# Tail columns scaled on ScalarE and summed by transposes in PSUM, with 384 dense cells a head and an exponential ranking of the keys

## The chip, the cores and the metric

The kernel runs on one core of a Trainium2 chip, in one launch. The metric is the device time of a run in microseconds. The kernel before took 1063.42 us, the median of three runs (1061.2 to 1066.42). Engines are named as in the profile: PE is TensorE (matmuls and transposes) with its weight load PEld, DVE is VectorE, ACT is ScalarE, POOL is GpSimd (it issues the gathers), SP is SyncE (it issues the other transfers).

## The reference

One encoder layer works on 512 tokens of width 1024, all in float32. A mixer comes first (windowed attention and latent attention side by side, with norms that a conditioning vector modulates); the change leaves it alone. Then comes PEER, a retrieval over 128 x 128 experts of one neuron each, and a last RMSNorm. PEER, per token `x` (after its norm), with 8 heads and two halves `p` of the query:

```
q     = (x @ w_query)                       # 8 heads x 2 halves x 128
s     = q . sub_keys[head, half]            # 128 scores for each half
top_s, top_i = top_k(s, 16)                 # 16 keys of each half
cand  = top_s[0][:, None] + top_s[1]        # 256 pairs; pair (i, j) is expert 128 i + j
best_s, idx  = top_k(cand, 16)              # 16 experts a head, 128 a token
g     = softmax(best_s)
out   = sum over head, k of  g * gelu(x . expert_u[idx]) * expert_v[idx]
x     = x + g_f * out ;  result = rmsnorm(x, final_norm)
```

A row of `expert_u` with its row of `expert_v` is 8 KB.

## The kernel before

**Dense and tail.** Which expert a token wants is known only at run time, and 512 x 128 pairs of token and expert are too many to gather one by one. Some experts are wanted by many tokens, so the kernel ranks the 128 keys of each half by how often they lie high, and takes a fixed staircase of ranks, `RECTS` (L32), as the dense cells: key ranks `a0` to `a1` of one half with the first `w` ranks of the other. That makes 512 cells, experts, a head. They are computed for all 512 tokens by matmul: each head has 4 chunks (`NCH`) of 128 experts. What a token wants outside the cells is its tail.

**Ranking** (`rank1` to `rank3`, L1198 to L1245). Before a head's scores exist, `rank1` scores the first 128 tokens only (L1204), takes each token's eighth largest score with VectorE's max, and marks the keys at or above it; `rank2` counts the marks by matmuls with ones (L1213, L1215), compares the counts pair by pair into ranks, and turns ranks into a permutation matrix `pm`; `rank3` permutes the keys (L1231) and stores the table of expert ids and the ids of the cells.

**Routing** (`route`, L1427). Written out by hand as one list of steps, in which the head `i` is scored, head `i+1` is ranked, head `i+2` gets its query, and head `i-1` has its weights made: the dense weights `dexp` of 512 cells for each token, masked, transposed (L1419) and stored to DRAM as `gts`, and the other pairs as a list of expert code and weight a token (`cdgs`, in DRAM `cdg`). `dn(k)` in it pulls one step of the dense work. `start_routing` (L1004) opens it: it ranks head 0 among the transposes that write the tokens to DRAM (`rows`, L1010, operation `tt<-ident,x1T` L1014), and runs head 1's query. At the end the tokens are sorted by the length of their tails.

**Dense work** (`dense`, L1497). A generator. For each chunk: gather 128 rows of u (`du`), transpose them in four 128x128 pieces (`turn`, L1522), round them to a high part `uh` (ScalarE, L1525) and a correction `ul` (`low`: L1532, then ScalarE L1533), 24 matmuls into `udot` (`dots`, L1540), gelu (ScalarE, L1545), times the weights `gT` (VectorE, L1553). Once the first chunk of the next head is through, `outputs` of a head (L1579) multiplies its 4 chunks of weights with its 4 gathered `dv` into `vacc` (L1591), 4 token blocks by 2 halves of 512 columns, and VectorE adds each to `accd` (L1565). `vacc` has two banks of PSUM pool `PD[0]` and, in the tail stage, one of `PD[1]`.

**Tail.** Sorted tokens make four blocks of 128. Column `j` of a block is the `j`-th tail expert of each of its tokens, `TAIL` (L37) says how many columns a block gets, and tokens with more pairs put the rest on rows of a shared block "fold" of 4 columns, which `fold_rows` (L1704) lays out and a matmul with `fold` brings home (`begin`, L1939). That is 81 columns. For each: GpSimd looks up 128 ids (`tid`) and gathers 128 rows of 8 KB into one of 6 buffers `tuv` (L156 from `tail_id` and `tail_load`). Then, with the gate found by L1882:

```
L1891  DVE  dot of tuv[:, 0:D] with the tokens hp        (tail_col)
L1811  ACT  gelu of the dot          (flush, one column later)
L1812  ACT  times the gate: wg
L1813  DVE  tacc = tuv[:, D:] * wg + tacc
```

At a block's end `add_tail` multiplies `tacc` by the layer gate `gf` (L2015), adds the residual rows `x1` (L2016) and scatters to DRAM `zs`. When the last block and the last head's outputs are done, `finish` (L2071) loads `zs`, joins it to `accd` (L2081), norms and stores.

**What sets the order.** In the tail stage each engine keeps the order in which the program issues (`in_order`, L1087). `interleave` (L1102) decides it: each step of `dense` adds its TensorE cost (`PE_CHUNK`, `PE_OUT`) to a meter, and columns are loaded (`t.load`) or worked (`t.col`) as their costs (`DM_COL`, `VE_COL`) fall due, at `RATE` 1.05 of an even spread. The steps that routing took are subtracted. `t.load` runs up to 5 columns ahead.

Of the kernel before, what the change touches and what calls it, by code (L numbers as in the profile page):

```python
# [31 lines left out]
RECTS = ((0, 2, 60), (2, 6, 31), (6, 14, 20), (14, 32, 6))  # L32
# [4 lines left out]
TAIL = (29, 21, 16, 11)  # L37
FOLD = 4
MOST = 56
# [19 lines left out]
PE_OUT = 3.43  # L59
# [4 lines left out]
VE_COL = 2.9  # L64
# [857 lines left out]
def peer(tc, A, G, DR, out, xpool):  # L922
    nc = tc.nc
    with ExitStack() as ctx:
# [55 lines left out]
        with ExitStack() as c2:  # L980
# [3 lines left out]
            G.vbufs.append(1)  # L984
# [19 lines left out]
def start_routing(tc, G, H):  # L1004

    nc = tc.nc
    with tc.tile_pool(name="h2p", bufs=1, side="right") as W:
# [9 lines left out]

        H[0].rank1()
        rows(0)
        H[0].rank2()  # L1020
        rows(1)
# [80 lines left out]
def interleave(t, dense, ready, used):  # L1102
# [21 lines left out]
    for p, d, v in dense:  # L1124
        load += p * rd - d
        vec += p * rv - v
        while (load > 0 or vec > 0) and t.ncol < NTAIL:
            if (load > 0 or t.nuv - t.ncol < 2) and t.nuv < min(NTAIL, t.ncol + len(t.uv) - 1):
# [13 lines left out]
    while t.ncol < NTAIL:  # L1142
        if t.nuv < min(NTAIL, t.ncol + len(t.uv) - 1):
            t.load()
# [7 lines left out]
def route_setup(tc, A, G, R):  # L1152
    nc = tc.nc
    G.onesb = R.tile([128, 128], BF16, name="onesb")
    nc.vector.memset(G.onesb, 1.0)
# [4 lines left out]
    G.noff = R.tile([128, 258], F32, name="noff")  # L1160
    iota(nc, G.noff[:, 0:256].rearrange("p (a b) -> p a b", a=2), [[0, 2], [1, 128]])
    iota(nc, G.noff[:, 256:258], [[0, 2]], cm=1)
# [5 lines left out]
class Head:  # L1168
# [28 lines left out]

    def rank1(self):  # L1198
        nc, R = self.nc, self.R
        pss = self.G.PS.tile([128, 2, 128], F32, name="pss", tag="rank")  # L1200
        m8 = R.tile([128, 2, 8], F32, name="m8s", bufs=2)
        self.ind = R.tile([128, 2, 128], BF16, name="ind", bufs=1)
        for p in range(2):
            nc.tensor.matmul(pss[:, p], self.q[p][:, 0:128], self.keys[:, 0, p], start=True, stop=True)  # L1204
        for p in range(2):
            nc.vector.max(m8[:, p], pss[:, p])
        for p in range(2):
            nc.vector.tensor_scalar(self.ind[:, p], pss[:, p], m8[:, p, 7:8], None, op0=OP.is_ge)

    def rank2(self):  # L1210
        nc, R, G = self.nc, self.R, self.G
        psc = G.PS.tile([128, 258], F32, name="psc", tag="rank")
        nc.tensor.matmul(psc[:, 0:256], G.onesb, self.ind.rearrange("p a b -> p (a b)"), start=True, stop=True)  # L1213
        for p in range(2):
            nc.tensor.matmul(psc[:, 256 + p:257 + p], self.ind[:, p], G.onesb[:, 0:1], start=True, stop=True)  # L1215
        key = R.tile([128, 258], F32, name="pkey", bufs=1)
# [898 lines left out]
```

## Time and profile before

| | us |
|---|---|
| runs | 1061.2, 1063.42, 1066.42 |
| profiled execution | 1053.43 |
| its span | 1051.6 |
| TensorE busy (89%) | 940.5 |
| VectorE busy (76%) | 794.0 |
| GpSimd busy (51%) | 534.5 |
| ScalarE busy (40%) | 424.5 |

The mean granted clock of TensorE is 0.961. HBM was read for 187.95 MB at 197 GB/s over the span with the writes. The span is one execution's time from first to last instruction, and the profiled execution's own time lies 1.8 us above it. The mixer takes the first 330 us or so; routing runs from there to 597 us; dense chunks and tail columns share the time from 597 to 1006 us; the last join and norm follow. Busy TensorE is not TensorE at its peak, as matmuls are pipelined and their ends are modelled: a group's mean there is more than the distance from one to the next.

### The profile page before, as it was taken

Reading aid. Unit: us, or ns where it says so; the run is one execution under the profiler, and the core shown is the slowest. Engines: PE = TensorE matmul, PEld = TensorE weight load, DVE = VectorE, ACT = ScalarE, POOL = GpSimd, SP = SyncE. Lnnn points to the kernel's source line nnn. Section 1 sums busy time; section 2 is a strip of 40 time slices with the busy share of each in tenths; the row PEclk is TensorE's granted clock in tenths of the full one; section 3 lists DMA queues with packets and bytes.
Section 4 is the critical chain, followed back from the end, with each engine's and each line's share of the span. In section 5 each row is a group of like instructions: output and inputs, shape, how many; then the busy total and the mean of one; then the engine's idle time right before and its main releaser. Section 6 shows DMA issues by size and latency. Waiting matters only on the chain.

```text
span 1051.6 us, 13224 instructions
## 1 busy us (share of the span) xinstructions
PE 940.5 (89%) x4046; PEld 619.5 (59%) x4046; DVE 794.0 (76%) x2284; ACT 424.5 (40%) x921; POOL 534.5 (51%) x553
## 2 busy tenths in 40 slices
PE   7898989998999898999878878999998999969992
PEld 2475648776898545666554454563746666555641
DVE  4628566889637379999999587998677886866987
ACT  2333366656414335577764332231413323122312
POOL 1145611324322144666665547687578857675513
PEclk9999899999999998999988989999999999989996
DMA  8554132422211643554325669977689869786542
GB/s 317 208 227 166 55 113 86 174 82 90 81 41 60 218 148 101 161 143 123 98 60 131 214 244 313 344 249 256 243 310 389 315 228 337 271 304 238 169 175 82
DMA packets 77189, 198.94 MB, mean 189 GB/s; under 512 B 23286, under 2 KB 41078, under 8 KB 64886
## 3 DMA queue, kind: packets, MB, share of 16 engines
q0 software_dynamic: 26400, 118.93, 31.6%
q1 hardware_dynamic: 49992, 78.50, 22.5%
q8 instruction: 32, 0.52, 0.2%
q10 hardware_dynamic: 720, 0.62, 0.2%
q14 instruction: 45, 0.37, 0.1%
HBM read 187.95 MB, written 18.96 MB: 197 GB/s over the span
## 4 chain that ended last, share of the span: by engine, by line
PE 59%; DVE 23%; DMA 6%; issue 5%; ACT 3%; POOL 2%; another core or an unknown queue 0%; SPq 0%; ACTq 0%; DVEq 0%; POOLq 0%
PE vacc L1591 13%; PE udot L1540 12%; PE q L1191 8%; PE proj L305 4%; PE outp L305 4%; PE ops L831 3%; DMA tuv<-in_UV,tid 3%; PE ut L1522 2%; PE sc L807 2%; DVE tscr L1891 2%; PE adar L352 1%; DVE tacc L1813 1%; PE pt L815 1%; PE ut L1532 1%; DMA wraw_pq<-in_w_pq 1%
## 5 line engine op out<-in xcount | busy, mean ns | idle before, releaser
L1591 PE MATMUL vacc<-dv,gT 128*128 128x512 f32 x512 | 229.2, 605 | 7.0 <-DVE accd L1565 5.7
L1591 PEld LDWEIGHTS vacc<-dv,gT 128*128 128x128 f32 x512 | 98.5, 194 | 129.8 <-issue 114.3
L1813 DVE SCALAR_TENSOR_TENSOR tacc<-tuv,twg,tacc 128x1024 f32<-128x1024 f32 x81 | 103.7, 1280 | 35.1 <-ACT twg L1812 28.0
L1891 DVE SCALAR_TENSOR_TENSOR tscr<-tuv,thp 128x1024 bf16<-128x1024 f32 x81 | 98.8, 1220 | 32.8 <-DMA tuv<-in_UV,tid 24.4
L156 POOL DMA_INDIRECT tid<-tab,tci x81 | 98.5, 1216 | 29.5 <-issue 23.0
L156 POOL DMA_INDIRECT tuv<-in_UV,tid x81 | 97.9, 1208 | 29.1 <-issue 16.4
L1540 PE MATMUL udot<-hH,uh 128*128 128x512 f32 x256 | 109.8, 429 | 0.0
L1540 PE MATMUL udot<-hH,ul 128*128 128x512 f32 x256 | 104.1, 407 | 0.0
L1540 PE MATMUL udot<-hL,uh 128*128 128x512 f32 x256 | 103.6, 405 | 0.0
L1191 PE MATMUL q<-hx,wraw_pq 128*128 128x512 f32 x208 | 95.8, 602 | 0.0
L1811 ACT ACTIVATE twg<-tdots 128x1 f32<-128x1 f32 x81 | 16.4, 202 | 140.1 <-DVE tscr L1891 124.7
L327 POOL TENSOR_TENSOR ada_acc<-ada_acc,ada_w 128x1024 f32<-128x1024 f32 x9 | 21.5, 2384 | 81.5 <-ACT ada_w L326 28.6
L297 POOL TENSOR_TENSOR wl_in<-wraw_in,wh_in 128x1024 fp32r<-128x1024 f32 x10 | 25.9, 2590 | 70.5 <-ACT wh_in L296 70.3
L1191 PEld LDWEIGHTS q<-hx,wraw_pq 128*128 128x128 f32 x208 | 38.2, 193 | 37.3 <-issue 36.9
L809 ACT ACTIVATE psb<-psb,anm 128x512 f32<-128x512 f32 (+2 forms) x64 | 41.0, 641 | 46.1 <-DVE psb L808 31.3
L1533 ACT CAST ul<-ut 128x512 fp32r<-128x512 f32 x64 | 37.4, 585 | 53.9 <-PE ut L1532 36.6
L1525 ACT CAST uh<-ut 128x512 fp32r<-128x512 f32 x64 | 37.3, 584 | 52.3 <-PE ut L1522 32.5
L1540 PEld LDWEIGHTS udot<-hH,ul 128*128 128x128 f32 x256 | 49.7, 194 | 12.5 <-issue 0.2
L1540 PEld LDWEIGHTS udot<-hH,uh 128*128 128x128 f32 x256 | 50.1, 196 | 9.4 <-issue 1.2
L1540 PEld LDWEIGHTS udot<-hL,uh 128*128 128x128 f32 x256 | 50.0, 195 | 9.4 <-issue 0.2
L156 POOL DMA_INDIRECT dv<-in_UV,cid x32 | 40.7, 1271 | 25.0 <-PE vacc L1591 16.9
L1532 PE MATMUL ut<-uh,nident 128*128 128x512 f32 x64 | 29.5, 461 | 24.3 <-issue 11.6
(402 smaller groups left out, 2211.9 us busy)
## 6 DMA issues: line engine op xcount, KB each, us to landing
ada_w<-in_w_ada SPq DMA_DIRECT2D x22, 1024.0 KB
wraw_pq<-in_w_pq SPq DMA_DIRECT2D x16, 512.0 KB
gts<-gts SPq DMA_DIRECT2D x32, 256.0 KB
gT<-gts SPq DMA_DIRECT2D x32, 256.0 KB
wraw_in<-in_w_in SPq DMA_DIRECT2D x10, 512.0 KB
wraw_out<-in_w_out SPq DMA_DIRECT2D x8, 512.0 KB
x1T<-in_xT SPq DMA_DIRECT2D x4, 512.0 KB
ada_w<-in_w_ada SPq DMA_DIRECT2D x4, 512.0 KB
```

The costliest lines, as they stand in the source:

```text
L156: nc.gpsimd.indirect_dma_start(out=out, out_offset=None, in_=src, in_offset=bass.IndirectOffsetOnAxis(ap=idx, axis=0), **kw)
L305: nc.tensor.matmul(ps, a[:, c], b[:, c], start=n == 0, stop=n == 3 * kc - 1)
L809: nc.scalar.activation(U.p, U.p, AF.Exp, bias=nm, scale=-1.0, accum_out=B.den[:, i:i + 1])
L831: nc.tensor.matmul(B.ops[U.grp][:, U.h], U.pt[:, j], vr, start=j == 0, stop=j == U.nk - 1)
L1191: nc.tensor.matmul(self.q[p][:, cols], w[:, c], x[:, c, cols], start=c == 0, stop=c == KC - 1)
L1525: nc.scalar.copy(uh, pt)
L1532: nc.tensor.matmul(pt, G.nident, uh, start=False, stop=True, skip_group_check=True)
L1533: nc.scalar.copy(ul, pt)
L1540: nc.tensor.matmul(ps, a, b[:, k], start=k == 0 and i == 0, stop=k == KC - 1 and i == 2)
L1591: nc.tensor.matmul(ps, ws[h, k][:, b * 128:(b + 1) * 128], vs[k][:, sl], start=k == 0, stop=k == NCH - 1)
L1813: nc.vector.scalar_tensor_tensor(acc, uv[:, D:], wg, acc, op0=OP.mult, op1=OP.add)
L1891: nc.vector.scalar_tensor_tensor(B.s, uv[:, 0:D], 1.0, B.hp, op0=OP.mult, op1=OP.mult, accum_out=B.dots[:, c])
```

## The change

Four things are changed together.

1. `RECTS` now has five steps and 384 cells a head, so `NCH` is 3: 24 dense chunks in all, and three products instead of four in each `vacc`. `TAIL` becomes 34, 26, 20, 14, with 4 fold columns as before: 98 columns, and up to 64 pairs a token.
2. The ranking. `rank0` scores all 512 tokens against the 128 keys of a half in one product, keys on partitions, and ScalarE takes the exponential with the sum over the tokens (`stat`). `rank1` reads the sum's bits as an integer, shifts it, and subtracts a small offset to part ties; `rank2` turns the copies of the keys to rows by two transposes and ranks as before. The max, the marks and the counting matmuls are gone.
3. The sums of the tail. `flush` has ScalarE multiply the gathered v half in place by `wg`; one column later `sum_late` turns its eight 128x128 pieces on TensorE into two PSUM banks `tsum`, which add up a block's columns (transposed). Only the 4 fold columns keep VectorE's accumulation. At a block's end `end_sums` copies the eight pieces with the gate `gfc` on ScalarE, turns them back on TensorE into the `vacc` banks, and VectorE adds the result to the residual rows. Fold rows come home by eight 128-column products a block, into the same banks.
4. What follows from it: `vacc` has only the two banks of `PD[0]`; there are 7 buffers `tuv`, with the same lead of 5; the next head's u are loaded earlier; the costs `PE_OUT` and `VE_COL` are 2.6 and 2.1; `rank2` stands behind `dn(1)`.

```diff
-RECTS = ((0, 2, 60), (2, 6, 31), (6, 14, 20), (14, 32, 6))
+RECTS = ((0, 2, 45), (2, 6, 23), (6, 14, 12), (14, 25, 6), (25, 45, 2))
-TAIL = (29, 21, 16, 11)
+TAIL = (34, 26, 20, 14)
-MOST = 56
+MOST = 64
-PE_OUT = 3.43
+PE_OUT = 2.6
-VE_COL = 2.9
+VE_COL = 2.1
...
+        H[0].rank0(0)
+        rows(0)
+        H[0].rank0(1)
+        rows(1)
         H[0].rank1()
-        rows(0)
         H[0].rank2()
-        rows(1)
         H[0].rank3()
...
+    def rank0(self, p):
+        ps = self.G.PS.tile([128, T], F32, name="pst", tag="rank")
+        nc.tensor.matmul(ps, self.keys[:, 0, p], self.q[p], start=True, stop=True)
+        nc.scalar.activation(junk, ps, AF.Exp, scale=KEYSCALE, accum_out=self.stat[:, p:p + 1])
...
+        nc.vector.tensor_scalar(bits, self.stat.bitcast(I32), KEYBITS, None, op0=OP.arith_shift_right)
+        nc.vector.tensor_tensor(self.key, bits, G.noff, op=OP.subtract)
...
-                i = 0 if len(G.PD) == 1 or (b * 2 + hh) % 3 else 1
-                ps = G.PD[i].tile([128, 512], F32, name="vacc", bufs=G.vbufs[i])
+                ps = G.PD[0].tile([128, 512], F32, name="vacc", bufs=2)
...
-    for uv, wg, dot, gate, acc in t.pending:
+    for uv, wg, dot, gate, acc, pe in t.pending:
         nc.scalar.activation(wg, dot, AF.Gelu)
         nc.scalar.activation(wg, wg, AF.Copy, scale=gate)
-        nc.vector.scalar_tensor_tensor(acc, uv[:, D:], wg, acc, op0=OP.mult, op1=OP.add)
+        if pe:
+            nc.scalar.activation(uv[:, D:], uv[:, D:], AF.Copy, scale=wg)
+            t.late.append((uv, acc))
+        else:
+            nc.vector.scalar_tensor_tensor(acc, uv[:, D:], wg, acc, op0=OP.mult, op1=OP.add)
...
+def sum_late(nc, G, t):
+    for uv, S in t.late:
+        for hh in range(2):
+            for k in range(4):
+                o = D + (hh * 4 + k) * 128
+                nc.tensor.matmul(S.ps[hh][:, k], uv[:, o:o + 128], G.ident, is_transpose=True, start=not S.open and k == 0,
...
     nc.vector.scalar_tensor_tensor(B.s, uv[:, 0:D], 1.0, B.hp, op0=OP.mult, op1=OP.mult, accum_out=B.dots[:, c])
+    if t.late:
+        sum_late(nc, t.G, t)
     flush(nc, t)
...
+    for k in range(KC):
+        nc.scalar.activation(turned[:, k], S.ps[k // 4][:, k % 4], AF.Copy, scale=G.gfc[:, k:k + 1])
+    yield
+    G.flush_adds()
+    back = [G.PD[0].tile([128, 4, 128], F32, name="tback", tag="vacc", bufs=2) for _ in range(2)]
+    for k in range(KC):
+        nc.tensor.transpose(back[k // 4][:, k % 4], turned[:, k], G.ident)
+    yield
+        nc.vector.tensor_tensor(x1[:, sl], x1[:, sl], back[hh].rearrange("p j t -> p (j t)"), op=OP.add)
```

On TensorE the start of routing stood so before. `pss` are the scores of 128 tokens for the ranking of head 0, `tt` the turned tokens, `psk` the permuted keys, `q` the query of head 1, `sps` the scores of head 0:

```order
L1204 MATMUL pss<-keys,qsb 128x128 x2
L1014 MATMUL tt<-ident,x1T 128x128 x8
...
L1014 MATMUL tt<-ident,x1T 128x128 x4
L1231 MATMUL psk<-pm,keys 128x128 x2
L1014 MATMUL tt<-ident,x1T 128x128 x4
L1232 MATMUL psk<-prow,pm 128x1
L1233 MATMUL psk<-pm,prow 128x128
L1191 MATMUL q<-x1T,wraw_pq 128x512 x4
L1263 MATMUL sps<-kp,qsb 128x128 x4
```

There after the change, from the first `tt` on (`pst` are the ranking scores of all tokens; the first `pst` stands just ahead):

```order
L1017 MATMUL tt<-ident,x1T 128x128 x4
L1193 MATMUL q<-x1T,wraw_pq 128x512
L1017 MATMUL tt<-ident,x1T 128x128 x4
L1206 MATMUL pst<-qsb,keys 128x512
L1017 MATMUL tt<-ident,x1T 128x128 x4
L1193 MATMUL q<-x1T,wraw_pq 128x512
L1017 MATMUL tt<-ident,x1T 128x128 x4
L1224 MATMUL psc<-ident,pkeyb 128x128 x2
L1193 MATMUL q<-x1T,wraw_pq 128x512 x2
L1238 MATMUL psk<-pm,keys 128x128 x2
```

Head 1's query now stands in pieces between the steps of head 0's ranking, and the first of them ahead of the second rank product.

At the outputs of the first head of the tail stage, TensorE's order was, from the last dots of the chunk on:

```order
L1540 MATMUL udot<-hH,uh 128x512
L1540 MATMUL udot<-hL,uh 128x512
L1540 MATMUL udot<-hH,ul 128x512
L1591 MATMUL vacc<-dv,gT 128x512 x32
L1522 MATMUL ut<-ident,du 128x128 x4
```

And it is now, at the same place (the number of `tuv` is that of its buffer):

```order
L1549 MATMUL udot<-hH,uh 128x512
L1549 MATMUL udot<-hL,uh 128x512
L1549 MATMUL udot<-hH,ul 128x512
L1837 MATMUL tsum<-ident,tuv_5684 128x128 x8
L1599 MATMUL vacc<-dv,gT 128x512 x3
L1837 MATMUL tsum<-ident,tuv_5685 128x128 x8
L1599 MATMUL vacc<-dv,gT 128x512 x3
L1837 MATMUL tsum<-ident,tuv_5686 128x128 x8
L1599 MATMUL vacc<-dv,gT 128x512 x3
```

An output has three products instead of four, and the eight transposes of a column stand between one output and the next.

At the last head's outputs, behind which TensorE has nothing left to do, stood `vacc<-dv,gT` x32 in one piece, from the last dots on:

```order
L1540 MATMUL udot<-hL,uh 128x512
L1540 MATMUL udot<-hH,ul 128x512
L1591 MATMUL vacc<-dv,gT 128x512 x32
L987 TENSOR_LOAD nit
L988 COMPARE_AND_BRANCH
```

Now the last three columns' transposes and those that turn the last sums back (`tback`) stand behind the first output:

```order
L1549 MATMUL udot<-hH,ul 128x512
L1837 MATMUL tsum<-ident,tuv_5684 128x128 x8
L1599 MATMUL vacc<-dv,gT 128x512 x3
L1837 MATMUL tsum<-ident,tuv_5685 128x128 x8
L1837 MATMUL tsum<-ident,tuv_5686 128x128 x8
L1837 MATMUL tsum<-ident,tuv_5687 128x128 x8
L2061 MATMUL tback<-ident,tturn 128x128 x8
L1599 MATMUL vacc<-dv,gT 128x512 x21
L990 TENSOR_LOAD nit
```

Seven of the eight outputs wait behind the last columns.

## Rows read from the trace of the kernel before

**Rows 1.** The chain that ended last, by engine, whole span.

```profile
PE 59%; DVE 23%; DMA 6%; issue 5%; ACT 3%; POOL 2%; another core or an unknown queue 0%; SPq 0%; ACTq 0%; DVEq 0%; POOLq 0%
```

**Rows 2.** Stretches of the span, busy time of each engine; columns by the header.

```profile
core 0: us, PE busy (x) PEld busy (x) DVE busy (x) ACT busy (x) POOL busy (x), PEclk, DMA share, GB/s
428.00:521.00 93.00, 92.98 (x406) 60.31 (x405) 89.36 (x507) 63.80 (x118) 55.83 (x105) 1.00 0.51 143
521.00:597.00 76.00, 57.53 (x217) 34.05 (x215) 67.27 (x294) 43.98 (x75) 45.17 (x75) 0.89 0.38 103
...
597.00:1005.80 408.80, 374.65 (x1320) 233.65 (x1320) 321.34 (x599) 113.63 (x297) 271.10 (x225) 0.97 0.78 282
793.50:826.90 33.40, 29.63 (x137) 23.88 (x136) 26.80 (x49) 13.31 (x32) 27.30 (x21) 0.95 0.97 367
1005.80:1051.60 45.80, 26.02 (x60) 11.31 (x60) 35.99 (x70) 8.51 (x22) 14.42 (x10) 0.82 0.30 116
```

**Rows 3.** Chain of waits in order of time: start us, us, what.

```profile
511.28 0.44 PE ut L1522 x4
513.12 6.87 PE q L1191 x16
519.99 0.23 PE ut L1532
520.21 1.40 PE udot L1540 x6
521.61 0.46 PE pss L1204 x4
...
701.77 27.48 PE vacc L1591 x64
```

**Rows 4.** Groups, 597 to 1005.8 us: count | busy, mean ns | idle before, releasers.

```profile
L1591 PE MATMUL vacc<-dv,gT 128*128 128x512 f32 x388 | 170.8, 598 | 5.7 <-DVE accd L1565 5.7
L1813 DVE SCALAR_TENSOR_TENSOR tacc<-tuv,twg,tacc 128x1024 f32<-128x1024 f32 x79 | 101.1, 1280 | 35.0 <-ACT twg L1812 28.0 <-ACT twg L1811 6.5 <-issue 0.4
L156 POOL DMA_INDIRECT tuv<-in_UV,tid x81 | 97.9, 1208 | 29.1 <-issue 16.4 <-DVE tacc L1813 5.4 <-DVE gT L1553 2.7
L1891 DVE SCALAR_TENSOR_TENSOR tscr<-tuv,thp 128x1024 bf16<-128x1024 f32 x80 | 97.6, 1220 | 32.8 <-DMA tuv<-in_UV,tid 24.4 <-issue 7.9 <-DVE gT L1553 0.2
...
L1540 PE MATMUL udot<-hH,uh 128*128 128x512 f32 x214 | 91.5, 428 | 0.0
...
L1882 DVE SCALAR_TENSOR_TENSOR tjunk<-tcd,tcode 128x400 bf16<-128x400 f32 x60 | 38.1, 635 | 0.0
...
L1522 PE MATMUL ut<-ident,du 128*128 128x128 f32 x204 | 32.1, 282 | 0.0
...
L1532 PE MATMUL ut<-uh,nident 128*128 128x512 f32 x52 | 22.4, 430 | 24.3 <-issue 11.6 <-ACT uh L1525 8.4 <-ACT act L1545 2.3
```

**Rows 5.** TensorE in order of time, start of routing: start us, us, operation, count.

```profile
351.88 0.47 PE L1233 MATMUL psk<-pm,prow 128*128 128x128 f32 x2
352.84 3.70 PE L1191 MATMUL q<-x1T,wraw_pq 128*128 128x512 f32 x8 [0.49 <-DMA wraw_pq<-in_w_pq]
```

**Rows 6.** All heads' score products: durations ns, first and last start us.

```profile
L1263 PE MATMUL sps<-kp,qsb x128: 271/275/377, 356.4 to 538.5; 128*128 128x128 f32 x128
```

**Rows 7.** Groups of the whole span, ScalarE's fill of 128x1024.

```profile
L1805 ACT ACTIVATE tuv<-gf 128x1024 f32<-128x1024 f32 x6 | 5.8, 1045 | 6.8 <-DVE code L1823 6.8
```

**Rows 8.** GpSimd's gathers into tuv: min/median/max ns, first and last start us.

```profile
L156 POOL DMA_INDIRECT tuv<-in_UV,tid x81: 986/992/2024, 596.4 to 996.0; - x81
```

**Rows 9.** VectorE in order of time at the end of the last column.

```profile
1006.30 1.22 DVE L1891 SCALAR_TENSOR_TENSOR tscr<-tuv,thp 128x1024 bf16<-128x1024 f32 x1
...
1018.16 0.69 DVE L1568 TENSOR_TENSOR vgf<-vacc,gf 128x512 f32<-128x512 f32 x1 [1.55 <-PE vacc L1591]
...
1019.80 1.23 DVE L2081 TENSOR_TENSOR accd<-accd,tuv 128x1024 f32<-128x1024 f32 x1 [0.23 <-DMA tuv<-zs]
```

**Rows 10.** Transposes pt (mixer's attention) from 216 to 271 us.

```profile
216.00:271.00 55.00, 13.66 (x84) 1.00 0.26 87
```

More of the change, by code (lines that the diff above doesn't have):

```diff
@@ L1439, in route @@
     on(L, "best", 0, 0)
+    on(N, "rank0", 0)
     on(L, "best", 0, 2)
@@ L1599, in outputs @@
             values((h + 1) * NCH)
-    for c in range(4):
+    for c in range(NCH):
         load_u(c)
@@ L1608, in dense @@
         yield PE_CHUNK / 4, 0.0, 0.0
-    load_u(4)
+    for c in range(NCH, 5):
+        load_u(c)
     vs = {}
@@ L1795, in tail_setup @@
     t.k = 0
-    t.pending = []
+    t.pending, t.late = [], []
     t.loaded = []
@@ L1891, in tail_col @@
     nc.vector.scalar_tensor_tensor(B.s, uv[:, 0:D], 1.0, B.hp, op0=OP.mult, op1=OP.mult, accum_out=B.dots[:, c])
+    if t.late:
+        sum_late(nc, t.G, t)
     flush(nc, t)
-    t.pending = [(uv, B.wg[:, c], B.dots[:, c], B.gate[:, c], acc)]
+    t.pending = [(uv, B.wg[:, c], B.dots[:, c], B.gate[:, c], acc, pe is not None)]
 def tail(tc, A, G, TL, out):
     nc = tc.nc
-    G.tl = t = tail_setup(tc, TL, 6)
+    G.tl = t = tail_setup(tc, TL, 7)
+    t.G = G
+    G.flush_adds()
+    gp = G.PD[0].tile([128, KC], F32, name="gfcp", tag="vacc", bufs=2)
+    for k in range(KC):
+        nc.tensor.matmul(gp[:, k:k + 1], G.gf[:, k * 128:(k + 1) * 128], G.ident[:, 0:1], start=True, stop=True)
+    G.gfc = TL.tile([128, KC], F32, name="gfc")
+    nc.scalar.copy(G.gfc, gp)
     G.fold = TL.tile([128, NB, 128], F32, name="fold")
@@ L1927, in begin, with add_fold @@
     def begin(i):
[L1929 to L1944 removed]
+        S = accs[i]
+        S.ps = [G.PD[1].tile([128, 4, 128], F32, name="tsum", bufs=2) for _ in range(2)]
+        if "fold" in accs:
+            add_fold(i)
+    def add_fold(i):
+        S = accs[i]
+        for hh in range(2):
+            for k in range(4):
+                o = (hh * 4 + k) * 128
+                nc.tensor.matmul(S.ps[hh][:, k], accs["fold"][:, o:o + 128], G.fold[:, i], start=not S.open and k == 0,
+                                 stop=False, skip_group_check=True)
+        S.open = True
     cols = [(i, j) for i in TORDER for j in range(FOLD if i == "fold" else TAIL[i])]
@@ L1978, in col @@
         i, j = cols[n]
+        prev = cols[n - 1 - j][0] if n > j else None
         if j == 0:
-            flush(nc, t)
-            if n and cols[n - 1][0] == "fold":
-                begin(TORDER[0])
-            t.acc = begin(i)
-        tail_col(tc, t, blocks[i], j, t.acc)
+            if i == "fold":
+                t.acc = accs[i] = TL.tile([128, D], F32, name="tacc", bufs=1)
+                nc.vector.memset(t.acc, 0.0)
+            else:
+                t.acc = accs[i] = State()
+                t.acc.open = False
+                if prev is None:
+                    begin(i)
+        ends = prev is not None and i != "fold"
+        if ends and j == 2:
+            next(t.end)
+            begin(i)
+        tail_col(tc, t, blocks[i], j, t.acc, None if i == "fold" else t)
+        if ends and j == 1:
+            if prev == "fold":
+                add_fold(TORDER[0])
+            t.end = end_sums(tc, G, TL, accs[TORDER[0] if prev == "fold" else prev], TORDER[0] if prev == "fold" else prev)
+            next(t.end)
+        if ends and j in (2, 4):
+            next(t.end, None)
         if n + 1 < len(cols):
             tail_gate(nc, blocks[cols[n + 1][0]], cols[n + 1][1])
-        if n > j and i != "fold":
-            k = TORDER[TORDER.index(i) - 1]
-            if j == ENDS[0]:
-                t.end = end_block(tc, G, TL, accs, TORDER[0] if k == "fold" else k)
-            if j in ENDS:
-                next(t.end, None)
         t.ncol += 1
@@ L1996, in done @@
         flush(nc, t)
-        for _ in end_block(tc, G, TL, accs, TORDER[-1]):
+        sum_late(nc, G, t)
+        for _ in end_sums(tc, G, TL, accs[TORDER[-1]], TORDER[-1]):
             pass
```

100 lines of the change are left out of this document (45 added, 55 removed).

## Prediction, made before the changed kernel was run

> **What bounds the kernel now.** I read the chain of waits first, then stretches of the span, then groups and waits of the stretch that the change rebuilds. The chain that ended last is 59% TensorE and 23% VectorE [rows 1]. The stretches say where each holds. From 428 to 521 us (routing of heads, with the first dense chunks) TensorE is busy 92.98 of 93.00 us. From 521 to 597 us, where the last heads are routed and the tokens sorted, TensorE is busy 57.53 of 76 and VectorE 67.27: a VectorE chain. From 597 us to 1005.8 us (tail columns interleaved with the rest of the dense part, 408.8 us, the tail stage below) TensorE is busy 374.65, VectorE 321.34, GpSimd 271.10, ScalarE 113.63, and transfers run at 282 GB/s with a share of 0.78. The last 45.8 us are the final head's outputs, joins and norms [rows 2].
>
> Busy is not work for TensorE, so I price the tail stage by distances on the chain, where its instructions follow without a gap. 16 query half-matmuls took 6.87 us, so a half of an fp32 512-column matmul (the trace holds two of each) is 0.43; six udot matmuls 1.40, so 0.234 each; a correction (uh with nident) 0.23; four transposes 0.44, so 0.11 each; 64 vacc halves 27.48, so 0.429 [rows 3]. Times the counts of the tail stage [rows 4]: 388 x 0.429 + 642 x 0.234 + 204 x 0.11 + 52 x 0.234, and 8 us for the fold (16 halves of 0.43 and some small ones), is 359 us. So 50 of the 408.8 us are loss. TensorE's largest waits there stand at the correction, for issue 11.6 and for uh of ScalarE 8.4, and at vacc, 5.7 for a PSUM bank that VectorE empties [rows 4], and the mean granted clock of 0.97 makes about 12 more.
>
> **The change part by part.**
>
> Start of routing. Before, ranking of head 0 finished (its last product at 351.88) just as head 1's query weights landed, and TensorE went on with them at 352.84 [rows 5]. In the changed order a query matmul stands after the first four transposes, ahead of the second rank product and all that hangs on it. So from 352.84 on must still run: two rank halves 0.86, three times four transposes 1.3, two transposes of the keys 0.2, eight key products at 0.11, 0.9, the exponential and VectorE's steps in part exposed, about 1.0. Four query matmuls of 0.86 stand in either order before the second scores. About +3.4 us; bounds 0 (if VectorE's next chain swallows it) and 4.3.
>
> Each later round. Two rank products of 512 columns (1.72) and two transposes (0.22) come; four halves of 128 columns (0.46 by the row [rows 3]), the old counts (0.17) and four of the 16 transposes of the weights (0.44) go: +0.87 a round. From the first head's scores to the last's, seven rounds take 182.1 us [rows 6], 26.0 each, so the 93 us that TensorE bounds hold 3.6: +3.2. VectorE loses the two maxima and comparisons, and its masks shrink to three quarters; that matters from 521 to 597 us, where a fourth round of maxima for 26 codes and a seventh buffer to clear (1.04 on ScalarE [rows 7]) come on the chain. I take 0, bounds -4 and +3. One more small store a head goes through SyncE's queue, off the chain.
>
> The tail stage on TensorE, to the last head's first output. The steps of dense work given out during routing fix what is left: 18.25 chunks (26.75 before) and the outputs of six heads. Dots 18.25 x (24 x 0.234 + 2 x 0.234 + 8 x 0.11) = 127. Outputs 6 x 8 x 3 x 0.858 = 124. Column transposes: 94 of the 98 columns go through TensorE (the four folded ones don't), three of them after this point: 91 x 8 x 0.11 = 80. Fold products 32 x 0.215 = 7, turning back and the rest 4. Sum 342 against 359: -17 us. The 17 more columns and the turning thus eat most of the 109 us that a quarter of the dense part is worth.
>
> VectorE. A column falls from 1.28 + 1.22 + 0.64 to 1.86 us; the accumulation is gone for 94 of them [rows 4]. Its cover is that TensorE lost only 5.7 us on VectorE's adds and some 5 on fold products: I take -6. What is late next: the gather, in front of which the dot still stands.
>
> ScalarE gets a pass of 128x1024 a column, 1.04 us by the fill of the same size [rows 7] (the pass itself is not in the trace; bounds 0.5, half the fill, and 1.28, VectorE's pass of that size [rows 4]). 98 us fit beside its 114 us of work. But behind each stand the casts uh that TensorE waits for: 36 of them, up to 1.5 us late each, with some 0.7 us of slack as six udot matmuls lie between. I take +4, bounds 0 and +35. At the ends of blocks eight scaled copies stand between the column sums and the next block's first transpose: +3. Two output banks instead of three: +1, bounds 0 and +8, as VectorE's adds stand behind dots that waited 24 us for gathers.
>
> Gathers. Counted on the reference's inputs, token-expert pairs outside the dense cells rise from 9026 to 11097 (8 KB each: +17.0 MB), while 15 fewer gathers of 0.52 MB and 7 fewer loads of 0.26 MB remain: 115.3 + 7.3 = 122.6 MB in some 396 us, 310 GB/s. The trace held 367 GB/s over 33 us [rows 2], so it can be hidden. GpSimd issues 242 gathers instead of 225; at 1.21 us and a gap of 0.30 (between the idle time put down to issue, 16.4/81, and all of it, 29.1/81 [rows 4]) that is 364 us, under 396 by little. I take +2 for both, bounds -5 and +39.
>
> On that pitch a page has a word. A column's gather is issued in 0.99 us at the median and 2.02 at the longest [rows 8]. The Trainium skill (SBUF — State Buffer, "Who interferes with whom") says that VectorE's copies and the like lock GpSimd out of the port it needs for descriptors, while operations on two tensors take only the read side, which it infers leaves descriptors alone. By that, with no such copies beside them, the 242 gathers would take 242 x 1.29 = 312 us and never pace; by the rows, where the slow ones lie beside two-tensor operations, 364.
>
> The end. The last sums need a chain: gelu and gate 0.5, scaled pass 1.04, transposes 0.9, eight copies 2 (0.25 each: an eighth of the fill's 1.04, and as much again fixed, an estimate), turning back 0.9; and TensorE now holds seven of the eight outputs behind it. Before, the first join began 12 us after the last dot's end (1007.5 to 1019.8 [rows 9]), just behind VectorE's steps on the fourth output; now four outputs (4 x 2.57) after 5.3 us of chain, plus 1.7 for VectorE's two steps on the last of them, give 17. From the join on nothing changes. +5, bounds 0 and +9.
>
> Sum: 3.4 + 3.2 + 0 - 17 - 6 + 4 + 3 + 1 + 2 + 5 = -1.4 us on the profiled execution of 1053.43 us (span 1051.6). That execution is 10 us under the median of 1063.42, so I carry the difference: **1062 us**.
>
> **Rivals.**
> 1. VectorE's relief frees more than 6 us. Place: the tail stage, where VectorE was busy 321 of 409 us and holds gates, weighing and PSUM adds in one queue. If its share falls to two thirds, the losses of 50 us may shrink to 30: 20 us less, 1042. For it: GpSimd and TensorE waited on VectorE in many small pieces. Against: the two largest named waits, issue and uh, are not VectorE's.
> 2. Gathers pace the stage: slower. Place: GpSimd's queue and the transfers, needed at 310 GB/s where the whole stage ran at 282. It decides as soon as the rate stays under 307. At 295 GB/s 122.6 MB take 416 us, +20: 1082; at 282, 435 us, +39: 1101. For it: in the stretch with a share of 0.97 TensorE was busy 29.63 of 33.40 us. Against: that stretch held 367 GB/s [rows 2].
> 3. The clock falls. From 216 to 271 us TensorE did 84 transposes, 13.66 us of the 55, at a granted clock of 1.00 [rows 10], the 2.4 GHz level; in the tail 80 of some 396 us will be transposes. If a tenth of the stage ran at the lower level: +39 us at most by time, half of it lost, 1082.
> By a page of the Trainium skill (TensorE: Matmul & The Clock Gate, "Part 4: PE-mode transpose") transposes do not count as busy for the clock as matmuls do, which speaks for this rival; by that rule the output phases would fall first. The trace so far disagrees at that density, so it gets little.
> 4. The change overflows: the loop for left-over pairs runs. On the inputs the fold needs 119 rows of 128 and the longest token has 51 pairs of 64, so only a ranking off by much would do it: above 1100.
>
> **How the numbers follow.** Forecast 0.42 (1050 to 1072), rival 1 0.26, rival 2 0.21, rival 3 0.07, rival 4 0.04. A measurement here tells about 0.5%, 5 us, from no change. The forecast's spread lies 0.18 faster, 0.17 same, 0.07 slower; rival 1 adds 0.24 and 0.02; rivals 2 to 4 0.30 slower and 0.02 same. Faster 0.42, same 0.21, slower 0.37. For 8 in 10 the range reaches from rival 1 with some more of its bound, 1034, to between rival 2's two times, 1091.
>
> **What would show it.** The rank product's second half after 353 us; rounds of 26.9 us; a tail stage near 396 us with VectorE busy about 250 and ScalarE 215; transposes at 0.11 us; first join 17 us after the last dot. The prediction is wrong if TensorE's waits in the tail stage are over 70 or under 35 us, if the rate stays near 282 GB/s, or if a long stretch has a clock of 0.5.

## The result, and the profile after

The changed kernel took 1095.88 us (median of four runs, 1091.0 to 1108.25), the kernel before 1062.31 beside it: a ratio of 1.0351 with an interval of 1.0295 to 1.0407. I had forecast 1062 us, no change, and 1034 to 1091 as the range: the time lies 5 us outside. The size depends on the chip (the first one's number isn't recorded). On chip 7 the same two kernels stood at 1048.13 and 1034.45, 1.0125 (1.0064 to 1.0185). The profiled execution of the first result took 1108.25 us, 17 us more than the fastest run (granted clock 0.931 against 0.940), so it is used here for what waits on what, and lengths of stages are read from two later executions of the unaltered changed kernel.

From the page of the changed kernel, its costliest groups (busy us, mean ns | idle before, releaser), to be held against [rows 4]:

```profile
L1917 DVE SCALAR_TENSOR_TENSOR tscr<-tuv,thp 128x1024 bf16<-128x1024 f32 x98 | 119.7, 1222 | 76.1 <-DMA tuv<-in_UV,tid 53.9
L1837 PE MATMUL tsum<-ident,tuv 128*128 128x128 f32 x752 | 103.0, 282 | 8.2 <-ACT tuv L1824 7.2
L1824 ACT ACTIVATE tuv<-tuv,twg 128x1024 f32<-128x1024 f32 x94 | 108.3, 1152 | 3.1
L1541 PE MATMUL ut<-uh,nident 128*128 128x512 f32 x48 | 26.3, 547 | 59.9 <-issue 33.3
L159 POOL DMA_INDIRECT dv<-in_UV,cid x24 | 25.9, 1081 | 55.0 <-PE vacc L1599 49.7
```

VectorE's accumulations are gone, as foreseen, and ScalarE's pass takes 1.15 us. But VectorE's dots now wait 53.9 us for gathered columns (24.4 before), TensorE's correction waits 59.9 us (24.3 before), and GpSimd stands 49.7 us at the gather of `dv`, until TensorE's last output frees a buffer (16.9 before). That third wait is the one that I had not read.

Where the time stands by stage, from the first and last starts of the named tiles (us; the gather is the first of `tuv`, the dot the last of L1917 or L1891):

| | before, first chip | changed, chip 14 | changed, chip 7 |
|---|---|---|---|
| profiled execution | 1053.43 | 1075.58 | 1051.32 |
| first query product of head 0 | 329.7 | 342.1 | 340.0 |
| first scores of head 0 | 356.4 | 368.8 | 366.8 |
| seven rounds | 182.1 | 185.8 | 185.8 |
| last scores to first gather | 57.9 | 58.9 | 58.9 |
| first gather to end of last dot | 411.1 | 414.4 | 392.2 |
| last dot to end | 44.1 | 45.8 | 45.8 |

The same stretches as [rows 2], changed kernel on chip 14 (columns as there):

```profile
core 0: us, PE busy (x) PEld busy (x) DVE busy (x) ACT busy (x) POOL busy (x), PEclk, DMA share, GB/s
430.00:521.00 91.00, 91.00 (x370) 57.28 (x371) 80.53 (x442) 59.88 (x126) 58.48 (x124) 1.00 0.46 129
521.00:613.50 92.50, 75.00 (x275) 45.47 (x274) 78.07 (x391) 46.13 (x94) 47.50 (x95) 0.85 0.36 95
613.50:1027.90 414.40, 366.10 (x1749) 256.83 (x1748) 259.49 (x594) 211.30 (x406) 281.65 (x243) 0.95 0.82 293
1027.90:1073.70 45.80, 22.50 (x68) 10.66 (x66) 29.87 (x67) 11.80 (x32) 14.19 (x10) 0.78 0.32 116
```

And the tail stage on chip 7:

```profile
611.40:1003.70 392.30, 360.76 (x1746) 252.97 (x1744) 259.50 (x594) 209.35 (x405) 279.54 (x243) 0.97 0.85 309
```

VectorE at 259 and ScalarE at 210 are what I had said (250, 215). TensorE has lost only 10 to 15 us of its busy time.

At the start of routing, TensorE in order of time in the changed kernel on chip 7 (start us, us):

```profile
339.97 16.74 PE L1193 MATMUL q<-x1T,wraw_pq 128*128 128x256 f32 x64 [4.21 <-DMA wraw_pq<-in_w_pq]
357.38 1.13 PE L1206 MATMUL pst<-qsb,keys 128*128 128x512 f32 x2 [0.68 <-ACT qsb L1196]
...
366.78 1.05 PE L1270 MATMUL sps<-kp,qsb 128*128 128x128 f32 x8
```

And in the kernel before, whose last 23 products of that query stand behind the mixer as one piece:

```profile
329.73 1.03 PE L1191 MATMUL q<-x1T,wraw_pq 128*128 128x256 f32 x4
330.81 0.60 PE L1191 MATMUL q<-x1T,wraw_pq 128*128 128x256 f32 x2
332.02 2.84 PE L1191 MATMUL q<-x1T,wraw_pq 128*128 128x256 f32 x12
335.70 10.14 PE L1191 MATMUL q<-x1T,wraw_pq 128*128 128x256 f32 x46
```

Nine of head 0's 32 query products (18 of 64 halves) ran in the mixer's gaps before; now all 32 stand behind it, after a wait of 4.21 us for their weights. Counted from the mixer's last product (`outp`, at 329.4 us before and 328.9 here), the first scores come after 27.0 us before and after 37.9 here.

### The profile page after: what moved, and what is told of

Same layout as the page of the kernel before. It is cut to its first block, busy times and chain, and to the rows that moved or that the text cites. A ratio compares the mean times of both kernels' runs of the same rounds, so it can differ in the third digit from the quotient of the medians.

```text
span 1106.4 us, 14430 instructions
## 1 busy us (share of the span) xinstructions
PE 946.1 (86%) x4454; PEld 652.3 (59%) x4454; DVE 716.0 (65%) x2263; ACT 519.8 (47%) x1069; POOL 535.8 (48%) x602
## 5 line engine op out<-in xcount | busy, mean ns | idle before, releaser
L1599 PE MATMUL vacc<-dv,gT 128*128 128x512 f32 x384 | 182.4, 617 | 8.8 <-DVE accd L1572 8.8
L1917 DVE SCALAR_TENSOR_TENSOR tscr<-tuv,thp 128x1024 bf16<-128x1024 f32 x98 | 119.7, 1222 | 76.1 <-DMA tuv<-in_UV,tid 53.9
L1599 PEld LDWEIGHTS vacc<-dv,gT 128*128 128x128 f32 x384 | 71.7, 199 | 80.4 <-issue 69.4
L1837 PEld LDWEIGHTS tsum<-ident,tuv 128*128 128x128 f32 x752 | 92.2, 147 | 39.8 <-issue 22.2
L1837 PE MATMUL tsum<-ident,tuv 128*128 128x128 f32 x752 | 103.0, 282 | 8.2 <-ACT tuv L1824 7.2
L1824 ACT ACTIVATE tuv<-tuv,twg 128x1024 f32<-128x1024 f32 x94 | 108.3, 1152 | 3.1
L1574 DVE TENSOR_TENSOR accd<-accd,vacc 128x512 f32<-128x512 f32 x48 | 33.0, 687 | 89.6 <-PE vacc L1599 86.4
L1549 PE MATMUL udot<-hH,uh 128*128 128x512 f32 x192 | 85.5, 445 | 0.0
L1549 PE MATMUL udot<-hL,uh 128*128 128x512 f32 x192 | 80.9, 421 | 0.0
L1549 PE MATMUL udot<-hH,ul 128*128 128x512 f32 x192 | 80.6, 420 | 0.0
L1541 PE MATMUL ut<-uh,nident 128*128 128x512 f32 x48 | 26.3, 547 | 59.9 <-issue 33.3
L159 POOL DMA_INDIRECT dv<-in_UV,cid x24 | 25.9, 1081 | 55.0 <-PE vacc L1599 49.7
L308 PE MATMUL outp<-hH,ws_out 128*128 128x256 f32 x256 | 49.4, 287 | 0.0
```

What stands on the lines that cost most here:

```text
L159: nc.gpsimd.indirect_dma_start(out=out, out_offset=None, in_=src, in_offset=bass.IndirectOffsetOnAxis(ap=idx, axis=0), **kw)
L308: nc.tensor.matmul(ps, a[:, c], b[:, c], start=n == 0, stop=n == 3 * kc - 1)
L1541: nc.tensor.matmul(pt, G.nident, uh, start=False, stop=True, skip_group_check=True)
L1549: nc.tensor.matmul(ps, a, b[:, k], start=k == 0 and i == 0, stop=k == KC - 1 and i == 2)
L1574: nc.vector.tensor_tensor(dst, dst, ps, op=OP.add)
L1599: nc.tensor.matmul(ps, ws[h, k][:, b * 128:(b + 1) * 128], vs[k][:, sl], start=k == 0, stop=k == NCH - 1)
```

## The experiments

Times are medians, beside the kernel before on the same chip; a ratio stands with its 95% interval where there is one.

**The ranking alone** (chip 1). The kernel before with the four ranking parts of the diff:

```diff
+        H[0].rank0(0)
...
+        nc.scalar.activation(junk, ps, AF.Exp, scale=KEYSCALE, accum_out=self.stat[:, p:p + 1])
```

> The kernel before with the exponential ranking alone (512 cells, 81 columns, sums on VectorE). The first theory (the ranking costs TensorE 0.87 us a round and some 3 us at the start) expects 1066 to 1070. The rival (the ranking is nearly free, as the trace of the changed kernel has seven rounds in 183.1 us against 182.1, and the better ranking leaves 670 fewer tail pairs to move) expects 1058 to 1064.

1038.93 to 1035.65, 1.006 (1.0019 to 1.0102): by the ratio the first theory's answer, as its 1066 to 1070 are 1.003 to 1.007 of the kernel before on the first chip. Its rounds take 185.1 us, 3.0 more than before.

**The sums alone** (chip 1). The kernel before with `flush`, `sum_late`, `end_sums` and two output banks, 512 cells and 81 columns (the cuts are marked):

```diff
+            nc.scalar.activation(uv[:, D:], uv[:, D:], AF.Copy, scale=wg)
+            t.late.append((uv, acc))
...
-                ps = G.PD[i].tile([128, 512], F32, name="vacc", bufs=G.vbufs[i])
+                ps = G.PD[0].tile([128, 512], F32, name="vacc", bufs=2)
```

> The kernel before with the column sums on ScalarE and TensorE alone (512 cells, 81 columns, old ranking; the buffers of the rounded halves of u are 3 instead of 4 to make room). If the sums are what makes the tail stage long (TensorE's corrections waited 60 us instead of 20 behind ScalarE's pass and its own transposes), it is slower by 25 us and more than the 75 us of transposes that TensorE gets, that is 1140 or above. If the 98 columns and their gathers are the cause, it costs only the transposes less what VectorE gives back: 1090 to 1125.

1.0573 (1.0534 to 1.0611), 1093.72. The second answer, at its upper end: the transposes, and little else. Its tail stage is TensorE's:

```profile
602.10:1038.60 436.50, 426.04 (x1966) 294.79 (x1965) 234.26 (x526) 208.44 (x398) 245.23 (x224) 0.99 0.72 263
```

**384 cells with VectorE's sums** (chip 1). The changed kernel with the old `flush` and `begin`:

```diff
-        if pe:
-            nc.scalar.activation(uv[:, D:], uv[:, D:], AF.Copy, scale=wg)
-            t.late.append((uv, acc))
...
+        nc.vector.scalar_tensor_tensor(acc, uv[:, D:], wg, acc, op0=OP.mult, op1=OP.add)
```

> The changed kernel with the columns summed on VectorE as before (384 cells, 98 columns, exponential ranking, three output banks, 6 buffers). If the sums on ScalarE and TensorE are the cause of the loss, TensorE has 80 us less to do and the time falls under the kernel before, 1030 to 1055. If the gathers of 98 columns or VectorE (98 x 3.14 us a column) pace the stage, it stays at 1075 to 1100.

1.053 (1.0475 to 1.0586), 1089.56: the second answer, and by its ratio above that too. Without the sums on TensorE the kernel is slower still, as 98 columns stand on VectorE:

```profile
615.90:1045.00 429.10, 314.84 (x937) 180.82 (x938) 371.81 (x690) 98.18 (x291) 304.04 (x243) 0.86 0.79 282
```

VectorE is busy 371.81 of 429 us, and TensorE with 60 us less to do waits. So each half of the change costs over 5% by itself on this chip, one through TensorE and one through VectorE, and together (next run) they nearly cancel.

**The place in memory** (chip 1). `cand`, `dexp` and `gts` of 384 cells are 5 KB a partition smaller, and the pools behind them move. The changed kernel with that room left empty:

```diff
+            nc.vector.memset(G.R1.tile([128, 1280], F32, name="pad")[:, 0:1], 0.0)
```

> The changed kernel with 5 KB of unused space in the first pool of routing, so that the query weights lie where they lay before. In the order 9 of head 0's 32 query matmuls then stand among the mixer's last steps again. If their late start is what moved the first scores from 356.4 to 368.6 us, beside the ranking's own 3 to 4, the time falls by 5 to 8 us, to 1083 to 1091. If VectorE's later chain swallows it, it stays at 1091 to 1100.

1.0081 (1.0039 to 1.0122), 1041.08. The order is that of before again, here in a padded kernel on chip 7, with 23 products as one piece and the rest in the mixer's gaps:

```profile
334.33 10.15 PE L1194 MATMUL q<-x1T,wraw_pq 128*128 128x256 f32 x46
345.15 1.13 PE L1207 MATMUL pst<-qsb,keys 128*128 128x512 f32 x2 [0.68 <-ACT qsb L1197]
...
357.68 1.05 PE L1271 MATMUL sps<-kp,qsb 128*128 128x128 f32 x8
```

Alone the time told little, as the unaltered kernel had not run on that chip. So:

**The changed kernel again**, on chips 9, 14 and 7:

> The changed kernel unaltered, to stand on the same chip as the others. The padded one ran at 1.008 of the kernel before. If the place of the query weights is all that the padding mends (first scores 6 us earlier), this one stands at 1.013 to 1.018. If the padding also mended the tail stage (447 us in its trace, 392 in the padded one's), or if its first runs were made where TensorE's signals came up to 10 us late, it tells by the tail stage: 392 with a ratio of 1.015 says it was the chip of the first runs, 430 or above with a ratio of 1.035 says it is the layout.

> The changed kernel unaltered, beside the padded one on one chip. Layout theory: it is slower than the padded one by 6 to 10 us on any chip (query weights alone). Rival, that the padding also mends the tail stage: 20 us or more, with a tail stage longer by 15 or more. Its ratio to the kernel before is 1.03 to 1.04 where TensorE's signals come late (waits named remote on ScalarE's uh over 10 us), and 1.012 to 1.018 where they don't.

> The changed kernel unaltered once more. Where no signal of TensorE comes late: 1.012 to 1.020 of the kernel before (the padded one's 1.008 and 5 to 10 us for the query weights). Where they come late: 1.03 to 1.04 as before.

1091.03 against 1048.66, and 1095.55 against 1049.87 (their runs lie from 1073 to 1099, and neither has an interval); on chip 7 1.0125 (1.0064 to 1.0185), at the low end of what I had written.

**The padded kernel again** (chip 14):

> The padded kernel again. 1.008 of the kernel before where TensorE's signals come in time (no wait named remote); 1.02 to 1.03 where they come late, as the late signals then cost it about 15 us more than they cost the kernel before. If it stays at 1.008 with late signals, the layout was all of the loss.

1.0317 (1.0244 to 1.039), 1082.09, slower than I had expected there. The medians on that chip differ by 13 us, but the unaltered kernel's one run of 1075.58 is as fast as the padded one's fastest. On chip 7 the unaltered kernel stood 0.4% above what the padded one did on chip 1. Counted from the mixer's last product, whose own place moves from run to run, the first scores come after 27.0 us before, after 27.5 to 29.7 in the nine padded traces, and after 37.6 to 37.9 in the four unaltered ones. So the padding gives back 8 to 10 us of the start, which is shown; what that is worth at the end, some 5 us by the two chips, is not settled. It does not shorten the tail stage: on chip 1, in the padded kernel, that takes 392.1 us, on chip 7, in the unaltered one, 392.3; on chip 14 it is 428 against 414.

**The ranking alone again** (chip 9), the same kernel as the first:

> The ranking alone once more for one look on this chip: 1.003 to 1.009 of the kernel before, tail stage 388 to 394 us.

1064.89 (one run) against 1048.66, above the range, with a tail stage of 418.5 us. It shows a difference between the chips. ScalarE's waits in the tail stage that no engine's work explains, in this kernel on chip 9:

```profile
ACT uh L1533 <- remote: 14.7, 4, 5.7
ACT ul L1541 <- remote: 10.5, 3, 4.5
ACT act L1553 <- remote: 6.0, 2, 3.0
```

On chip 1 there are none, and the tail stage took 391.2 us there, with the same code. The kernel before had 18 us of them on the first chip, the unaltered changed kernel 27 on chip 9, 31 on chip 14 and none on chip 7. The kernel before itself ran at 1034 to 1036 us on chips 1 and 7, and at 1049 to 1062 on the others.

**Half the bytes** (chip 9):

```diff
-    gather(nc, uv, A["UV"], B.ids[:, j:j + 1], NEXP - 1)
+    gather(nc, uv[:, 0:D], A["UV"].rearrange("e (k d) -> (e k) d", k=2), B.ids[:, j:j + 1], NEXP - 1)
```

> The padded kernel with a column's gather bringing 4 KB rows instead of 8 KB (rows of one half only, and not those of the column's experts; the v half stays as it was cleared, so the sums are left out in value, all instructions run). It moves some 45 MB less in the tail stage with as many gathers. If the transfers pace the stage (my second rival), it falls by 15 us or more, to 1.00 less 0.01. If TensorE's own work and its waits for ScalarE do, it falls by less than 6 us. A fall of 6 to 15 would say both.

1.0218 (1.0139 to 1.0297), 1076.71. The padded kernel with whole rows did not run on this chip. The unaltered kernel did, 14 us slower, of which the padding's earlier start can be 8 to 10. In the traces the stage took 424 us at 179 GB/s with half the bytes, and 415 at 292 GB/s in the unaltered kernel: bytes do not pace the stage there.

**Thirty columns back to VectorE** (chip 9):

```diff
+        ve = i != "fold" and j > 3 and j % 5 in (1, 3)
+        tail_col(tc, t, blocks[i], j, t.acc.v if ve else t.acc, None if ve or i == "fold" else t)
```

> The padded kernel with 30 of the 94 columns summed on VectorE again (into one tile a block, whose eight pieces TensorE turns into the same banks at the block's end). TensorE loses 30 x 0.88 = 26 us and gains 3.5, ScalarE loses 30 x 1.15 = 35, VectorE gains 30 x 1.28 + 4 = 42 (258 to 300 of some 390 us). If TensorE's work bounds the stage, it falls by 15 to 22 us, to 0.985 to 0.993 of the kernel before. If VectorE's queue or the gathers bound it, it stays at 1.00 to 1.01.

1.011 (1.0046 to 1.0173): the second answer, at its edge (VectorE's queue or the gathers), and not TensorE's work. The run also had 3 instead of 4 buffers for `uh` and `ul`.

**Corrections a quarter chunk later** (chip 14), in the padded kernel and in the kernel before:

```diff
+        two = len(G.PD) == 2
         for k in range(4):
-            if c + 1 < n:
+            if c + 1 < n and two:
+                (low if k > 1 else turn)(c + 1, k % 2)
+            elif c + 1 < n:
                 (low if k % 2 else turn)(c + 1, k // 2)
```

> The padded kernel with the two corrections of a chunk moved one quarter of a chunk later on TensorE, so that 12 udot matmuls (2.8 us) instead of 6 lie between a half's transposes and its correction. If the loss is ScalarE's uh coming late to TensorE (60 us of waits at the correction in the changed kernel's first trace), the waits at the correction fall to a third and the time by 8 to 20 us against the padded one. If these waits only move to the next thing TensorE needs from ScalarE, it falls by less than 4.

> The same edit on the kernel before, whose waits at the correction were 24 us: 0.985 to 0.993 if they are lost time, 0.997 to 1.003 if VectorE or the gathers take their place.

Padded 1.027 (1.0211 to 1.0329), 4 us under the padded one beside it: TensorE's waits at the correction fell from 32 us to 7, and 20 for ScalarE's scaled columns came. Before 0.9902 (0.9842 to 0.9961): there it was lost time, on this chip.

**ScalarE's pass taken away** (chip 7):

```diff
-            nc.scalar.activation(uv[:, D:], uv[:, D:], AF.Copy, scale=wg)
```

> The padded kernel without ScalarE's pass over a column's v half (94 x 1.15 us; gates and gelu still computed, but the sums are of unscaled v). TensorE turns the same columns. If ScalarE's pass between the dot and TensorE, and in front of the casts uh, is what the tail stage loses by, it falls by 20 us or more, to 1.00 to 1.01 of the kernel before also where TensorE's signals come late. If TensorE's own transposes and the late signals behind them are, it falls by less than 8 us and stays at 1.02 to 1.03 there.

1.0009 (0.997 to 1.0049): 7 us under the padded kernel's ratio of chip 1. The chip had no late signals, so it tells only that the pass is not the main cost there.

**Seven of eight transposes taken away** (chip 7):

```diff
+                if S.open and (hh or k):
+                    continue
```

> The padded kernel with one of the eight transposes for every column but a block's first (seven eighths of the sums are left out; ScalarE's pass and all gathers stay). TensorE loses some 69 us of work. If TensorE's work and its late signals bound the stage, it falls by 40 us and more under the kernel before, to 0.96 to 0.98. If ScalarE's pass or the 98 gathers bound it, it falls by 10 to 20 only, to 1.00 to 1.02.

1.0001 (0.9968 to 1.0033): 8 us under the padded kernel's ratio of chip 1, for 69 us of TensorE's work. The tail stage of that padded kernel, and of this one:

```profile
609.50:1001.60 392.10, 358.04 (x1745) 252.16 (x1743) 259.34 (x594) 209.08 (x405) 274.56 (x243) 0.98 0.86 309
603.60:983.90 380.30, 313.19 (x1101) 193.49 (x1101) 259.08 (x594) 206.74 (x403) 272.79 (x243) 0.91 0.88 319
```

TensorE sits idle for 67 us and the stage is 12 us shorter. Its work is not the bound. GpSimd's wait at `dv` fell along with it, from 31.0 us in the padded kernel's trace to 21.7.

**A spare buffer for dv** (chip 7, twice), with 3 instead of 4 buffers for `uh` and `ul` to make room, in the padded kernel and, with the later corrections, in the kernel before:

```diff
-        vs[j] = DN.tile([128, D], F32, name="dv", bufs=NCH)
+        vs[j] = DN.tile([128, D], F32, name="dv", bufs=NCH + 1)
```

> The padded kernel with one more buffer for the gathered dv (and 3 instead of 4 for the rounded halves of u, to make room), so that GpSimd's gather for the next head doesn't wait for the last output of this one (49.7 us of GpSimd's waits in the changed kernel's trace, 16.6 before), with the column gathers queued behind it. If the starved columns are what TensorE then waits for, it falls by 8 to 20 us. If TensorE is behind for reasons of its own, GpSimd just waits elsewhere: under 4.

> The kernel before with the corrections a quarter chunk later (0.990 by the run so far) and one more buffer for dv as above: 0.980 to 0.988 if GpSimd's blocked queue costs the kernel before something too, 0.988 to 0.993 if not.

> The padded kernel with the spare buffer for dv again. Where no signal comes late: 0.983 to 0.991 of the kernel before, as on the last chip. Where they come late: if GpSimd's blocked queue is how late signals cost the changed kernel more (TensorE late at the last output, so dv late, so columns late), it stands at 0.99 to 1.005, under 1.01 in any case. If late signals hit TensorE and ScalarE directly, at 1.01 to 1.02.

The padded kernel with it stands at 0.9869 (0.9803 to 0.9934) and, beside the unaltered changed kernel's 1.0125, at 0.9839 (0.9781 to 0.9896): 1018.17 us against 1034.45 and 1048.13. That beats both kernels, by 1 to 2% the kernel before. The kernel before gets 0.9959 (0.9919 to 1.0) from both edits there, a smaller gain than either of my answers. GpSimd's gathers of `dv` in the tail stage, in the kernel before (first chip), in the unaltered kernel and in the one with the buffer, both on chip 7:

```profile
L156 POOL DMA_INDIRECT dv<-in_UV,cid x27 | 35.7, 1323 | 23.9 <-PE vacc L1591 16.6 <-issue 5.2 <-PE ut L1532 1.2
```

```profile
L159 POOL DMA_INDIRECT dv<-in_UV,cid x18 | 20.6, 1142 | 33.7 <-PE vacc L1599 29.8 <-issue 2.7 <-PE ut L1541 0.6
```

```profile
L159 POOL DMA_INDIRECT dv<-in_UV,cid x18 | 20.8, 1155 | 5.5 <-issue 4.3 <-PE vacc L1600 0.6 <-PE ut L1532 0.3
```

And VectorE's largest wait in the two (us, times, longest), with the stage of the second:

```profile
DVE tscr L1917 <- DMA tuv<-in_UV,tid: 107.7, 62, 7.1
```

```profile
DVE tscr L1918 <- DMA tuv<-in_UV,tid: 58.1, 39, 6.6
```

```profile
602.80:971.80 369.00, 352.39 (x1749) 250.30 (x1747) 260.00 (x594) 210.14 (x406) 275.39 (x243) 0.99 0.89 329
```

29 us of waiting in front of the gathers of `dv` are gone, VectorE's wait for columns falls by 50, and the stage by 23 us, from 392 to 369 (369 in the first run with the buffer too). The padding has no part in this, as the padded kernel alone had a stage of 392.1 and a wait of 31.0 us on chip 1.

## Why the prediction was wrong

**Start of routing, +3.4.** Failed: it is 10.6 to 10.9, counted from the mixer's last product. The ranking's own part came out at 1 or less: with the padding, or with the ranking alone, the start takes 27.5 to 27.9 us in all traces but one, and 27.0 before. What I left out is the query itself. Nine products of it lay in the mixer's gaps, and in the changed kernel none. It stood in the order before I predicted (23 products in a row before, 32 after), and I priced only the rows behind it. The diff does not touch that code; it shrinks three tiles, and with their room left empty the old order is back.

**Each later round, +3.2.** Right: the seven rounds took 3.7 us more on chips 14 and 7, and 1.0 on the first chip and chip 9. **From the last scores to the first gather, 0:** +1.0 on chips 14 and 7, within its bounds (2.5 on chip 9, 3.4 on the first). **The end, +5:** +1.7. The chain that I priced was right: the first join comes 16.8 us after the last dot (17 forecast, 12.3 before). Wrong was that nothing changes behind it: from that join to the end it is 29.1 us against 31.8.

**The tail stage, -17 - 6 + 4 + 3 + 1 + 2 = -13.** Failed, and in the step that I gave +2, the gathers. That the stage measured 392 us on chip 7, near my 396, is luck: another engine set it. My sum took TensorE as the bound and its losses as fixed; its work fell about as worked out, and that was worth next to nothing, since taking away 69 us more of it gave 8. I put GpSimd's 242 gathers at 364 us, "under 396 by little", as if it could issue them back to back, and read no wait in its queue. But at a head's end the gather of the next `dv` waits for TensorE's last output, and every column gather queues behind it. In the changed kernel on chip 7, from the first column gather to the last (611.4 to 993.4 us), GpSimd's queue has no other room: 276 us of its instructions, 70 us of gaps of 0.3 us between them, 29.8 of waiting at `dv` and 5.5 at the fold make up the 382. The last dot ends 10 us later. So the pitch was 1.43 us and not 1.51, which alone would have been 346 us, and it was the waits that I had at nothing. With the spare buffer the queue takes 355 us, of which 12 are waits. In the kernel before, on the first chip, it stood for 68 of 400 us: 34 at the scatter of a finished block, behind VectorE, 16.6 at `dv`. There the spare buffer and the later corrections together are worth 4 us on chip 7. VectorE's relief of 6 us was no relief, as it then waited 108 us for columns.

So the second rival came, in one of its two places. I had it decide by the rate, "as soon as the rate stays under 307". The rate was 309 on chip 7 and 293 on chip 14, and 329 with the spare buffer, and half the bytes did not help: the queue decides, not the bytes. The first rival, VectorE's relief, did not come. Nor did the third on chip 7: with all 752 transposes the granted clock of the stage was 0.97, and 0.99 with the spare buffer, as against 0.97 before. The rule of the Trainium skill that I weighed there (TensorE: Matmul & The Clock Gate, "Part 4: PE-mode transpose") would have had it fall; at this mix of transposes and matmuls the trace doesn't show it. In the first result's trace the stage's clock was 0.92, on chip 14 it was 0.95; the last section shows one place where it fell, behind a long wait of TensorE. On the gathers' pitch the Trainium skill (SBUF — State Buffer, "Who interferes with whom") infers that two-tensor operations leave descriptors alone, and I had given that little. The traces lean to it, weakly: with 75 fewer such operations in the stage (L1813) the column's gather kept its mean, 1208 ns in both [rows 4], but with the same operations it is 1132 ns in the run with the spare buffer.

**The difference between chips.** On chip 7 the parts outside the tail stage make +17 us (10.4 + 3.7 + 1.0 + 1.7, against the only trace of before, which is from the first chip; against the kernel before with a spare buffer, on chip 7, they make 18), and the difference of the medians is +13.7: there the tail stage is about even. On the first chip the whole is +34, so the stage lost about 17 there. Waits named remote go with the chips on which the kernel before is slower too, but more of them in the changed kernel do not explain it: it has 31 us of them on chip 14 and 27 on chip 9, where the kernel before with the new ranking has 31 too. GpSimd's wait at `dv` is longer on those chips (34 to 50 us in the changed kernel and the padded one, against 30 and 31 on chips 7 and 1). Why signals come late on those chips is open, and so is by which part the changed kernel is hit harder there: the spare buffer ran on a chip without them only.

## What to carry to other kernels

An engine that issues transfers in order can be a bound of its own: count its instructions times their pitch, and add every wait that stands in that queue, whoever it is for. When a change takes work from two busy engines and hands the pace to a third, what the two gain is not a term of the sum. And a smaller tile can change the order of code that the diff leaves alone: read the whole order.

## What the runs showed of the hardware

In the profiled execution of the first result, TensorE's transposes of `du` and the dots behind them are recorded from 838.77 to 840.8 us, yet ScalarE, which waits for nothing else that the trace shows, starts on them at 852.70:

```profile
852.70 0.59 ACT L1534 CAST uh<-ut 128x512 fp32r<-128x512 f32 x1 [10.00 <-remote]
```

On TensorE the correction behind it follows after 12.56 us in which nothing is recorded, and the matmuls after it stand 0.43 us apart instead of 0.23. The granted clock is 1.00 until 841 us (the 2.4 GHz level), 0.50 from 853.3 to 856.6 (the 1.2 GHz level), and 1.00 again from 860:

```profile
853.34 0.80 PE L1541 MATMUL ut<-uh,nident 128*128 128x512 f32 x1 [12.56 <-issue]
853.93 0.63 PE L1549 MATMUL udot<-hH,uh 128*128 128x512 f32 x1
854.36 0.63 PE L1549 MATMUL udot<-hL,uh 128*128 128x512 f32 x1
```

Transposes follow that clock as matmuls do: a column's eight took 0.87 us at 1.00 (from 837.90) and 1.70 at 0.50 (from 856.49).

Such waits appear in all kernels run on the first chip and on chips 9 and 14, the longest 12.6 us on ScalarE and 13.0 on VectorE, and in none on chips 1 and 7. ScalarE's scaled pass in place over 128x1024 takes 1.15 us, more than the fill of the same size [rows 7], which I had taken for it.
